# A GpSimd multiplication in the weight load and a two-part moving operand in the expert stage of a decoder layer

## The chip, the core and the metric

The kernel runs on one core of a Trainium2 chip. The time is device microseconds from the first to the last instruction of one execution as the runtime counts them, the median of three runs: 4055.59 us (4050.54 to 4057.15). The engines that matter are TensorE (PE in the profile, its weight loads PEld), VectorE (DVE), ScalarE (ACT), GpSimd (POOL) and the queue of SyncE (SP), which issues most of the loads. ACT and DVE can read the matmul accumulator (PSUM) and SBUF; POOL works here on SBUF alone, and it issues the indirect gathers and scatters of rows.

## What is computed

One decoder layer over 4096 tokens of width 1024. The change lies wholly in its last part, a mixture of 32 experts in which each token goes to two of them:

```
gate  = p_group * p_exp / sum(p_exp)                       # two experts per token
hid   = silu(ragged_dot(xs, w1)) * ragged_dot(xs, w3)      # 1024 -> 512, per expert
ys    = ragged_dot(hid, w2) * gate                         # 512 -> 1024
ffn   = segment_sum(ys, tok)
x     = x + gate2[:, None, :] * ffn                        # gate2 scales the 1024 columns
return rmsnorm(x, final_norm_w)
```

## The kernel before

Four phases run one after the other; only the last, `phase_d` (from about 2600 us on), is touched. Every float32 operand is split into a high part of reduced precision and a remainder (`split`: ACT copies the high part, L71; DVE subtracts, L72), and a product of two operands is three matmuls: high by high, high by low, low by high.

The experts are sorted by token count. Rank r of that order is given a fixed number of rows `CAPS[r]` at build time; what an expert has beyond it is done by a loop at the end whose trip count is found at run time. The order of work alternates ranks from both ends of the list: 0, 31, 1, 30, 2, 29 and so on, ending in the middle. An expert of more than 384 rows is done in chunks of two tiles of 128 rows; all others are one chunk. For the inputs used, ranks 14 to 24 have 235, 203, 200, 200, 186, 172, 171, 168, 151, 136 and 129 tokens (counted from the reference), and before the change each of these eleven had 240 rows.

For each chunk:

- `d_gather` (L1397, POOL) gathers the rows of the next chunk into one of three x buffers; `d_turn` transposes them on PE (L1413) and splits them into `xh` and `xl`.
- `load_expert` brings the weights in twelve blocks of 128x1024: eight of w1 and w3, four of w2. Each is loaded by SP into a raw buffer (L1333; five of these exist), split by ACT into `whD` (L71) and by DVE into `wlD` (L72). The split buffers are a ring of 27 for whatever is in use, and an expert needs 24, so a block can be split only when PE has used up one of the expert before. The four w2 blocks are issued by `load(r, 12)` at the head of the expert's first chunk.
- `d_hidden`: for caps over 128 the weights stand in PE and x moves (L1442 to L1444): four column blocks j, two weights, eight slices k of 128, three products each, 192 in all. Three PSUM buffers take these groups of 24. ACT applies silu to the w1 group (L1447), DVE multiplies by the w3 group (L1448) and the result is split into `hh` and `hl`.
- `d_acc`, `d_to` (POOL): gather of the accumulated rows `ag` from DRAM (L1490) and three small operations for the scatter's row numbers (L1503 to L1505).
- `d_rows`: per 128 rows and half of the 1024 columns twelve matmuls with w2 (L1535 to L1537), then two DVE instructions, `yg = py * gate * g2` (L1542) and `ag = ag + yg` (L1543), then a scatter of `ag` (`keep`, L1570, POOL).
- `d_norm`, `d_root`, `d_out`: one chunk later the finished rows are normalised (DVE L1380) and scattered to the output (L1381, POOL).

A scheduler that runs when the kernel is built sets the order of each engine's queue from its own estimate of times; `self.pin` asks it to keep an instruction in the written order; the rows of the queues below show what came of that. Each engine then works through its queue strictly in order, so an instruction that waits holds back all behind it.

Of the kernel before, what the change touches and what calls it, by code (L numbers as in the profile page):

```python
# [53 lines left out]
class Kern:  # L54
# [1091 lines left out]

    CAPS = [832, 512, 512, 480, 480, 448, 384, 352, 320, 320, 320, 288, 288, 288] + [240] * 11 + [P] * 7
    NC = 384  # L1150

    def phase_d(self):
        tc, nc, T = self.tc, self.nc, self.T
        caps = [min(c, T) for c in self.CAPS]
        with tc.tile_pool(name="D", bufs=2) as p:
# [65 lines left out]
            for i, s in enumerate(st):  # L1221
                nx = st[i + 1] if i + 1 < len(st) else None
                r = s["r"]
                if s["first"]:
                    k = order.index(r)
                    if k + 2 < len(order):
                        load_slots(k + 2)
                    load(r, 12)
                if i == 2:
                    li, limb, col = self.overflow(p, caps)  # L1230
                if nx:
                    self.d_gather(p, nx, ids)

                jobs = []
                if s["last"] and nx:
                    jobs += [lambda: load(nx["r"], 2)] * 4

                pv = st[i - 1] if i else None
                acc = [lambda t=t, m=m: self.d_acc(p, s, t, m, ids) for t, m in s["tiles"]]
                free = self.AGS - (len(pv["tiles"]) if pv else 0)  # L1240
                ends = [acc[:free], acc[free:] + [lambda: self.d_to(p, s, slots)]]
                if pv:
                    ends[0].insert(0, lambda: self.d_norm(p, pv))
                    ends[1].insert(0, lambda: self.d_root(p, pv))
                    ends[1][1:1] = [lambda q=q: self.d_out(p, pv, q) for q in range(len(pv["tiles"]))]
                self.d_hidden(p, s, ex[r], jobs[:2], ends)
                turn = self.d_turn(p, nx) if nx else []
                self.d_rows(p, s, ex[r], slots, turn, jobs[2:], nx is None)
# [78 lines left out]
    def load_expert(self, p, e, w):  # L1327


        nc = self.nc  # L1330

        def block(raw, src, dst, key, n):
            nc.sync.dma_start(raw.rearrange("p (k n) -> p k n", n=n), src)  # L1333
            hi, lo = self.wtile("whD"), self.wtile("wlD")
            self.split(hi[:, 0:1024], lo[:, 0:1024], raw)
            dst[key] = [t[:, 0:1024].rearrange("p (k n) -> p k n", n=n) for t in (hi, lo)]

        for a in range(2):
            for nm, src in (("w1", self.w1), ("w3", self.w3)):
                s = src[0, bass.ds(e, 1)].rearrange("o (k p) n -> p (o k) n", p=P)  # L1340
                for q in range(2):
                    raw = p.tile([P, 1024], F32, name="rawD", bufs=self.RAWS)
                    block(raw, s[:, 4 * q:4 * q + 4, 256 * a:256 * a + 256], w[nm], (a, q), 256)
                    yield
        s = self.w2[0, bass.ds(e, 1)].rearrange("o (k p) n -> p (o k) n", p=P)
        for k in range(4):
# [55 lines left out]
    def d_turn(self, p, s):  # L1402

        nc = self.nc
        s["xh"], s["xl"] = (p.tile([P, KD, self.NC], F32R, name=nm, bufs=1) for nm in ("xh", "xl"))
        steps = []
        o = 0
        for (t, m), x in zip(s["tiles"], s["x"]):
# [12 lines left out]
    def d_hidden(self, p, s, w, jobs, ends):  # L1421
# [11 lines left out]
                    f()  # L1433

        if s["rows"]:
            for j in range(4):
                ph = {}
                for nm in ("w1", "w3"):
                    ph[nm] = self.psum([P, 512], "ph", "pj")[:, 0:n]
                    for k in range(KD):  # L1440
                        hi, lo = (b[:, k % 4, 128 * (j % 2):128 * (j % 2) + 128] for b in w[nm][j // 2, k // 4])
                        nc.tensor.matmul(ph[nm], hi, xh[:, k, 0:n], start=(k == 0), stop=False)  # L1442
                        nc.tensor.matmul(ph[nm], hi, xl[:, k, 0:n], start=False, stop=False)  # L1443
                        nc.tensor.matmul(ph[nm], lo, xh[:, k, 0:n], start=False, stop=(k == KD - 1))  # L1444
                    if nm == "w1":
                        hs = p.tile([P, 512], F32, name="hs", bufs=2)[:, 0:n]
                        nc.scalar.activation(hs, ph[nm], AF.Silu)  # L1447
                nc.vector.tensor_tensor(hs, ph["w3"], hs, op=ALU.mult)  # L1448
                self.split(s["hh"][j][:, 0:n], s["hl"][j][:, 0:n], hs, nc.vector if j == 3 else None)
                if j % 2:  # L1450
                    job()
# [56 lines left out]
    def d_rows(self, p, s, w, slots, turn, jobs, last):  # L1508
# [14 lines left out]
        for q, (t, m) in enumerate(s["tiles"]):  # L1523
# [14 lines left out]

            def add(i):
                cs = slice(512 * i, 512 * i + 512)  # L1540
                yg = p.tile([P, 512], F32, name="yg", bufs=3)[0:m]
                nc.vector.scalar_tensor_tensor(yg, py[i], gate, self.g2[0:m, cs], op0=ALU.mult, op1=ALU.mult)  # L1542
                nc.vector.tensor_tensor(ag[0:m, cs], ag[0:m, cs], yg, op=ALU.add)  # L1543

            if q == 0:

# [73 lines left out]
```

## Time and profile before

| | |
|---|---|
| median of three runs | 4055.59 us |
| the profiled execution, its own time | 4068.07 us |
| its span, first to last instruction | 4066.3 us |
| mean granted TensorE clock | 0.979 |
| busy PE / PEld / DVE / ACT / POOL over the span | 95% / 86% / 63% / 39% / 38% |
| expert stage, 2640 to 4046 us: busy PE / DVE / ACT / POOL | 1364 / 1014 / 626 / 565 us of 1406 |

The profiled execution took 12.5 us more than the median, so differences worked out on it are carried over to the median. The busy shares are averages over stages; in the expert stage PE is busy almost throughout, and DVE is the next.

### The profile page before, as it was taken

Reading aid. Unit: us, or ns where it says so; the run is one execution under the profiler, and the core shown is the slowest. Engines: PE = TensorE matmul, PEld = TensorE weight load, DVE = VectorE, ACT = ScalarE, POOL = GpSimd, SP = SyncE. Lnnn points to the kernel's source line nnn. Section 1 sums busy time; section 2 is a strip of 40 time slices with the busy share of each in tenths; the row PEclk is TensorE's granted clock in tenths of the full one; section 3 lists DMA queues with packets and bytes.
Section 4 is the critical chain, followed back from the end, with each engine's and each line's share of the span. In section 5 each row is a group of like instructions: output and inputs, shape, how many; then the busy total and the mean of one; then the engine's idle time right before and its main releaser. Section 6 shows DMA issues by size and latency. Waiting matters only on the chain.

```text
span 4066.3 us, 72672 instructions
## 1 busy us (share of the span) xinstructions
PE 3853.1 (95%) x26602; PEld 3477.2 (86%) x26602; DVE 2550.0 (63%) x6629; ACT 1602.7 (39%) x3309; POOL 1565.0 (38%) x2195
## 2 busy tenths in 40 slices
PE   5999999999999999979999999599999999999997
PEld 4888888899999999967888888498888889888887
DVE  6655544477777777753444444657777777767786
ACT  3433343444544444432222222224444444444453
POOL 2333333234433443413444444423333443444443
PEclk9999999999999999989999999799999999999999
DMA  6444323422122122356555554446666676666673
GB/s 197 133 135 123 101 76 107 117 60 74 45 68 74 49 67 72 95 160 197 166 169 178 180 170 142 157 134 213 220 215 215 217 238 197 228 202 212 227 241 131
DMA packets 483393, 609.99 MB, mean 150 GB/s; under 512 B 101088, under 2 KB 381384, under 8 KB 483032
## 3 DMA queue, kind: packets, MB, share of 16 engines
q1 hardware_dynamic: 429400, 480.98, 38.4%
q0 software_dynamic: 50592, 118.90, 8.6%
q10 hardware_dynamic: 3040, 5.43, 0.5%
q8 instruction: 211, 3.46, 0.3%
q14 instruction: 150, 1.23, 0.1%
HBM read 475.20 MB, written 183.03 MB: 162 GB/s over the span
## 4 chain that ended last, share of the span: by engine, by line
PE 75%; DMA 9%; DVE 8%; issue 3%; ACT 3%; POOL 1%; SPq 1%; POOLq 0%; DVEq 0%; ACTq 0%
PE ph L1443 5%; PE ph L1444 5%; PE ph L1442 5%; PE pjB L533 4%; PE pjB L534 4%; PE pjB L535 4%; PE py L1535 3%; PE py L1536 3%; PE py L1537 3%; PE poC L298 3%; PE poC L299 3%; PE poC L297 3%; PE pgz L297 3%; PE pgz L299 3%; PE pgz L298 3%
## 5 line engine op out<-in xcount | busy, mean ns | idle before, releaser
L1442 PE MATMUL ph<-xh,whD 128*128 128x240 f32 (+7 forms) x2048 | 580.6, 289 | 14.5 <-DVE ssD L1363 6.5
L1443 PE MATMUL ph<-xl,whD 128*128 128x240 f32 (+7 forms) x2048 | 588.4, 288 | 1.3 <-DVE xl L72 0.8
L1444 PE MATMUL ph<-xh,wlD 128*128 128x240 f32 (+7 forms) x2048 | 586.6, 288 | 0.0
L71 ACT ACTIVATE whD<-rawD 128x1024 fp32r<-128x1024 f32 x384 | 401.3, 1056 | 309.9 <-PE py L1536 127.0
L72 DVE TENSOR_TENSOR wlD<-rawD,whD 128x1024 fp32r<-128x1024 f32 x384 | 460.8, 1218 | 31.2 <-ACT whD L71 30.0
L533 PE MATMUL pjB<-hhB,whi 128*128 128x260 f32 x1536 | 446.2, 293 | 9.9 <-DVE cv L541 5.1
L534 PE MATMUL pjB<-hlB,whi 128*128 128x260 f32 x1536 | 442.8, 289 | 2.6 <-DMA hlB<-hl_d 2.5
L535 PE MATMUL pjB<-hhB,wlo 128*128 128x260 f32 x1536 | 443.5, 289 | 0.0
L1442 PEld LDWEIGHTS ph<-xh,whD 128*128 128x128 f32 x2048 | 388.5, 191 | 20.3 <-ACT xh L71 8.4
L1443 PEld LDWEIGHTS ph<-xl,whD 128*128 128x128 f32 x2048 | 391.1, 191 | 5.9 <-DVE xl L72 3.6
L1444 PEld LDWEIGHTS ph<-xh,wlD 128*128 128x128 f32 x2048 | 391.0, 191 | 1.9
L533 PEld LDWEIGHTS pjB<-hhB,whi 128*128 128x128 f32 x1536 | 292.0, 191 | 14.1 <-ACT beta L410 5.3
L534 PEld LDWEIGHTS pjB<-hlB,whi 128*128 128x128 f32 x1536 | 292.8, 191 | 6.4 <-DMA hlB<-hl_d 3.9
L543 POOL TENSOR_TENSOR cv<-cv,cv 128x256 f32<-128x256 f32 x192 | 141.9, 740 | 405.5 <-DVE Xd L613 142.1
L535 PEld LDWEIGHTS pjB<-hhB,wlo 128*128 128x128 f32 x1536 | 292.8, 191 | 1.6
L1535 PE MATMUL py<-whD,hh 128*128 128x512 f32 (+4 forms) x640 | 258.6, 404 | 12.3 <-ACT hh L71 6.5
L1536 PE MATMUL py<-wlD,hh 128*128 128x512 f32 (+4 forms) x640 | 251.9, 394 | 0.0
L1537 PE MATMUL py<-whD,hl 128*128 128x512 f32 (+4 forms) x640 | 246.0, 400 | 2.9 <-DVE hl L72 2.6
L1570 POOL DMA_INDIRECT acc_d<-ag,to x80 | 111.9, 1399 | 343.1 <-DVE ag L1543 245.7
L541 DVE SCALAR_TENSOR_TENSOR cv<-pjB,cw,cv 128x256 f32<-128x256 f32 x384 | 183.1, 479 | 85.6 <-ACT cv L539 78.5
L299 PE MATMUL pgz<-whi,hlC 128*128 128x512 f32 x512 | 203.8, 398 | 9.7 <-DMA hlC<-hl_d 9.7
L297 PE MATMUL pj<-whi,hh 128*128 128x512 f32 x512 | 205.5, 401 | 6.3 <-ACT whi L71 6.3
(459 smaller groups left out, 10125.9 us busy)
## 6 DMA issues: line engine op xcount, KB each, us to landing
rawD<-in_w_dram SPq DMA_DIRECT2D x384, 512.0 KB, 5.5
wa<-in_w_ada_dram SPq DMA_DIRECT2D x48, 512.0 KB, 4.8
hhB<-hh_d SPq DMA_DIRECT2D x64, 260.0 KB, 4.0
hlB<-hl_d SPq DMA_DIRECT2D x64, 260.0 KB, 4.6
acc_d<-xC SPq DMA_DIRECT2D x32, 520.0 KB, 2.6
wraw<-in_w_in_dram SPq DMA_DIRECT2D x32, 512.0 KB, 6.5
hh_d<-hh SPq DMA_DIRECT2D x16, 1024.0 KB, 7.5
hl_d<-hl SPq DMA_DIRECT2D x16, 1024.0 KB, 10.1
```

The costliest lines, as they stand in the source:

```text
L71: nc.scalar.activation(hi, src, AF.Copy)
L72: (e_lo or nc.vector).tensor_tensor(lo, src, hi.bitcast(F32) if hasattr(hi, "bitcast") else hi, op=ALU.subtract)
L297: nc.tensor.matmul(out, a, hi, start=(k == 0), stop=False)
L299: nc.tensor.matmul(out, b, hi, start=False, stop=(k == KD - 1))
L533: nc.tensor.matmul(pj, wh, hh[k], start=(k == 0), stop=False)
L534: nc.tensor.matmul(pj, wh, hl[k], start=False, stop=False)
L535: nc.tensor.matmul(pj, wl, hh[k], start=False, stop=(k == KD - 1))
L1442: nc.tensor.matmul(ph[nm], hi, xh[:, k, 0:n], start=(k == 0), stop=False)
L1443: nc.tensor.matmul(ph[nm], hi, xl[:, k, 0:n], start=False, stop=False)
L1444: nc.tensor.matmul(ph[nm], lo, xh[:, k, 0:n], start=False, stop=(k == KD - 1))
L1535: nc.tensor.matmul(py[i], a, hi, start=(k == 0), stop=False)
L1536: nc.tensor.matmul(py[i], a, lo, start=False, stop=False)
```

## The change

- The caps of ranks 14 to 24 follow the token counts: one stays at 240, the ten others get 208 to 144.
- Where a chunk with rows on the moving side has at most 208 of them, `xh` and `xl`, now the two halves of one tile `xx`, pass behind the standing high part of the weight in one matmul of 2n columns; the product with the low part keeps n columns. So there are two products per slice instead of three. PSUM then holds two sums side by side; ACT copies the second to SBUF, DVE adds the first to it, and silu and the product read SBUF.
- POOL multiplies each raw w2 block by `g2` before it is split; for that, `d_rows` adds `py * gate` to `ag` in one DVE instruction, and the tile `yg` is gone.
- `load(r, 12)` is written behind the gather of the next chunk.

```
@@ -1146,7 +1146,7 @@
-    CAPS = [832, 512, 512, 480, 480, 448, 384, 352, 320, 320, 320, 288, 288, 288] + [240] * 11 + [P] * 7
+    CAPS = [832, 512, 512, 480, 480, 448, 384, 352, 320, 320, 320, 288, 288, 288] + [240, 208, 208, 208, 192, 176, 176, 176, 160, 144, 144] + [P] * 7
     NC = 384
     def phase_d(self):
@@ -1225,11 +1225,12 @@
                     k = order.index(r)
                     if k + 2 < len(order):
                         load_slots(k + 2)
-                    load(r, 12)
                 if i == 2:
                     li, limb, col = self.overflow(p, caps)
                 if nx:
                     self.d_gather(p, nx, ids)
+                if s["first"]:
+                    load(r, 12)
                 jobs = []
                 if s["last"] and nx:
@@ -1331,6 +1332,9 @@
         def block(raw, src, dst, key, n):
             nc.sync.dma_start(raw.rearrange("p (k n) -> p k n", n=n), src)
+            if n == D:
+                self.pin(nc.gpsimd.tensor_tensor(raw, raw, self.g2, op=ALU.mult))
             hi, lo = self.wtile("whD"), self.wtile("wlD")
             self.split(hi[:, 0:1024], lo[:, 0:1024], raw)
             dst[key] = [t[:, 0:1024].rearrange("p (k n) -> p k n", n=n) for t in (hi, lo)]
@@ -1402,7 +1406,8 @@
     def d_turn(self, p, s):
         nc = self.nc
-        s["xh"], s["xl"] = (p.tile([P, KD, self.NC], F32R, name=nm, bufs=1) for nm in ("xh", "xl"))
+        s["xx"] = p.tile([P, KD, 2, self.NC], F32R, name="xx", bufs=1)
+        s["xh"], s["xl"] = s["xx"][:, :, 0], s["xx"][:, :, 1]
         steps = []
         o = 0
         for (t, m), x in zip(s["tiles"], s["x"]):
@@ -1433,17 +1438,32 @@
                     f()
         if s["rows"]:
+            pair = n <= 208
             for j in range(4):
                 ph = {}
                 for nm in ("w1", "w3"):
-                    ph[nm] = self.psum([P, 512], "ph", "pj")[:, 0:n]
+                    ph[nm] = self.psum([P, 512], "ph", "pj")
+                    two = ph[nm][:, 0:2 * n].rearrange("p (a n) -> p a n", a=2) if pair else None
+                    ph[nm] = ph[nm][:, 0:n]
                     for k in range(KD):
                         hi, lo = (b[:, k % 4, 128 * (j % 2):128 * (j % 2) + 128] for b in w[nm][j // 2, k // 4])
-                        nc.tensor.matmul(ph[nm], hi, xh[:, k, 0:n], start=(k == 0), stop=False)
-                        nc.tensor.matmul(ph[nm], hi, xl[:, k, 0:n], start=False, stop=False)
+                        if pair:
+                            nc.tensor.matmul(two, hi, s["xx"][:, k, :, 0:n], start=(k == 0), stop=False)
+                        else:
+                            nc.tensor.matmul(ph[nm], hi, xh[:, k, 0:n], start=(k == 0), stop=False)
+                            nc.tensor.matmul(ph[nm], hi, xl[:, k, 0:n], start=False, stop=False)
                         nc.tensor.matmul(ph[nm], lo, xh[:, k, 0:n], start=False, stop=(k == KD - 1))
+                    hb = (p.tile([P, 512], F32, name="hs", bufs=2) if nm == "w1" else p.tile([P, 208], F32, name="hb", bufs=1) if pair
+                          else None)
+                    if hb is not None:
+                        hb = hb[:, 0:n]
+                    if pair:
+                        nc.scalar.activation(hb, two[:, 1], AF.Copy)
+                        nc.vector.tensor_tensor(hb, ph[nm], hb, op=ALU.add)
+                        ph[nm] = hb
                     if nm == "w1":
-                        hs = p.tile([P, 512], F32, name="hs", bufs=2)[:, 0:n]
+                        hs = hb
                         nc.scalar.activation(hs, ph[nm], AF.Silu)
                 nc.vector.tensor_tensor(hs, ph["w3"], hs, op=ALU.mult)
                 self.split(s["hh"][j][:, 0:n], s["hl"][j][:, 0:n], hs, nc.vector if j == 3 else None)
@@ -1538,9 +1558,7 @@
             def add(i):
                 cs = slice(512 * i, 512 * i + 512)
-                yg = p.tile([P, 512], F32, name="yg", bufs=3)[0:m]
-                nc.vector.scalar_tensor_tensor(yg, py[i], gate, self.g2[0:m, cs], op0=ALU.mult, op1=ALU.mult)
-                nc.vector.tensor_tensor(ag[0:m, cs], ag[0:m, cs], yg, op=ALU.add)
+                nc.vector.scalar_tensor_tensor(ag[0:m, cs], py[i], gate, ag[0:m, cs], op0=ALU.mult, op1=ALU.add)
             if q == 0:
```

Line numbers move: gather of x L1397 becomes L1401, gather of `ag` L1490 becomes L1510, its scatter L1570 becomes L1588, the output's L1381 becomes L1385, the low product L1444 becomes L1456, w2's products L1535 to L1537 become L1555 to L1557. The multiplication is L1337, the two-part product L1452, the new add L1463.

The first place is POOL's queue around the start of rank 20 (cap 240 before, 176 now), which follows rank 11 (288 rows, three tiles) and comes before rank 12. `acc_d<-ag` is the scatter of a finished tile, `ag<-acc_d` the gather of a new one, `out_dram` the output, `xg` a gather of x. Before:

```order
L1397 DMA xg<-h_d,ids 32x1024
L1570 DMA acc_d<-ag,to 4096x1040 x3
L1490 DMA ag<-acc_d,ids 128x1040
...
L1503 TENSOR_SCALAR to<-ag,slots 112x1
L1397 DMA xg<-h_d,ids 112x1024
...
L1570 DMA acc_d<-ag,to 4096x1040 x2
```

Now:

```order
L1401 DMA xg<-h_d,ids 32x1024
L1337 TENSOR_TENSOR rawD<-rawD,g_28189 128x1024 x4
L1588 DMA acc_d<-ag,to 4096x1040 x3
L1510 DMA ag<-acc_d,ids 128x1040
...
L1401 DMA xg<-h_d,ids 48x1024
L1337 TENSOR_TENSOR rawD<-rawD,g_28189 128x1024 x2
L1525 TENSOR_SCALAR to<-ag,slots 128x1
L1337 TENSOR_TENSOR rawD<-rawD,g_28189 128x1024 x2
...
L1523 TENSOR_SCALAR to<-ag,slots 48x1
L1588 DMA acc_d<-ag,to 4096x1040
```

The four multiplications for rank 20's w2 stand ahead of the three scatters of rank 11, and the four for rank 12's w2 stand ahead of the first scatter of rank 20, among its small operations.

The second place is PE's queue at the end of rank 20's hidden stage, where the last products of `ph` meet the transposes (`ptx`) and the first products with w2 (`py`; `hh` with the lowest number is j = 0). Before:

```order
L1442 MATMUL ph<-xh,whD 128x240
L1443 MATMUL ph<-xl,whD 128x240
L1444 MATMUL ph<-xh,wlD 128x240
L1413 MATMUL ptx<-K,xg 128x128 x8
L1535 MATMUL py<-whD,hh_41049 128x512
L1536 MATMUL py<-wlD,hh_41049 128x512
L1537 MATMUL py<-whD,hl_41053 128x512
L1535 MATMUL py<-whD,hh_41050 128x512
L1536 MATMUL py<-wlD,hh_41050 128x512
```

Now:

```order
L1452 MATMUL ph<-xx,whD 128x352
L1456 MATMUL ph<-xx,wlD 128x176
L1555 MATMUL py<-whD,hh_41600 128x512
L1556 MATMUL py<-wlD,hh_41600 128x512
L1555 MATMUL py<-whD,hh_41600 128x512
L1556 MATMUL py<-wlD,hh_41600 128x512
L1557 MATMUL py<-whD,hl_41604 128x512 x2
L1452 MATMUL ph<-xx,whD 128x352
```

The first products with w2 now stand among the hidden products, with two more column groups of 16 still behind them; before, they stood behind the last hidden product.

## Rows read from the trace of the kernel before

**Rows 1.** Windows: length, busy PE, PEld, DVE, ACT, POOL, clock, DMA share, GB/s

```profile
2640.00:4046.00 1406.00, 1364.38 (x9296) 1242.65 (x9294) 1013.76 (x1817) 625.63 (x936) 564.68 (x622) 0.99 0.64 209
3690.00:3708.00 18.00, 17.94 (x104) 14.27 (x103) 9.10 (x16) 1.35 (x3) 7.54 (x17) 1.00 0.37 124
3708.00:3741.00 33.00, 31.95 (x229) 27.84 (x228) 30.23 (x54) 20.09 (x31) 14.29 (x12) 1.00 0.79 260
```

**Rows 2.** PE's waits, 2640 to 4066: us in total, times, longest

```profile
PE ptx L1413 <- DVE xl L72: 10.3, 12, 1.5
...
PE plst L1320 <- DVE xl L72: 0.3, 1, 0.3
```

**Rows 3.** Timeline of PE, four widths: start and duration in us

```profile
3365.27 0.27 PE L1443 MATMUL ph<-xl,whD 128*128 128x240 f32 x1
...
3367.40 0.27 PE L1444 MATMUL ph<-xh,wlD 128*128 128x240 f32 x1
...
3183.14 0.27 PE L1444 MATMUL ph<-xh,wlD 128*128 128x192 f32 x1
...
3184.81 0.28 PE L1444 MATMUL ph<-xh,wlD 128*128 128x192 f32 x1
...
3830.71 0.29 PE L1444 MATMUL ph<-xh,wlD 128*128 128x288 f32 x1
...
3833.75 0.29 PE L1444 MATMUL ph<-xh,wlD 128*128 128x288 f32 x1
...
3245.30 0.34 PE L1444 MATMUL ph<-xh,wlD 128*128 128x384 f32 x1
...
3248.28 0.34 PE L1444 MATMUL ph<-xh,wlD 128*128 128x384 f32 x1
```

**Rows 4.** Groups of instructions: count, busy us, mean ns, idle before

```profile
L72 DVE TENSOR_TENSOR wlD<-rawD,whD 128x1024 fp32r<-128x1024 f32 x384 | 460.8, 1218 | 31.2 <-ACT whD L71 30.0
...
L1542 DVE SCALAR_TENSOR_TENSOR yg<-py,slots,g 128x512 f32<-128x512 f32 (+4 forms) x160 | 116.4, 747 | 133.6 <-PE py L1537 133.1
...
L1543 DVE TENSOR_TENSOR ag<-ag,yg 128x512 f32<-128x512 f32 (+4 forms) x160 | 107.6, 686 | 7.5 <-DMA ag<-acc_d,ids 3.8
...
L994 POOL TENSOR_TENSOR h2C<-h2C,B 128x1024 f32<-128x1024 f32 x31 | 74.2, 2395 | 39.6 <-DVE h2C L993 21.2 <-PE poC L299 8.8 <-DVE ohg L1026 3.9
```

**Rows 5.** Groups by shape: the steps behind a hidden group

```profile
L1448 DVE TENSOR_TENSOR hs<-ph,hs 128x224 f32<-128x224 f32 x8 | 3.1, 387 | 4.8 <-PE ph L1444 4.8
...
L1447 ACT ACTIVATE hs<-ph 128x192 f32<-128x192 f32 x4 | 1.3, 322 | 0.4 <-PE ph L1444 0.4
```

**Rows 6.** Timeline of the phase before, POOL and DVE

```profile
1976.37 2.40 POOL L994 TENSOR_TENSOR h2C<-h2C,B 128x1024 f32<-128x1024 f32 x1 [1.47 <-PE poC L299]
...
1976.82 3.10 DVE L72 TENSOR_TENSOR ml<-tr,mh 128x512 fp32r<-128x512 f32 x2 [0.60 <-ACT mh L71]
...
2002.18 1.28 DVE L72 TENSOR_TENSOR ml<-tr,mh 128x512 fp32r<-128x512 f32 x2
...
2178.02 1.29 POOL L947 TENSOR_TENSOR mix<-mix,sg 128x512 f32<-128x512 f32 x1 [3.87 <-ACT sg L940]
...
2178.76 1.29 DVE L979 TENSOR_TENSOR xC<-poC,xC 128x512 f32<-128x512 f32 x2 [0.45 <-DMA xC<-in_x_dram]
```

**Rows 7.** Timeline: a held POOL, a late scatter, a gap on PE

```profile
3658.70 4.58 POOL L1505 TENSOR_SCALAR to<-ag,slots 112x1 int32<-112x1 f32 x1
...
3671.12 1.28 DVE L1380 SCALAR_TENSOR_TENSOR ag<-ag,ssD,fw 128x1024 f32<-128x1024 f32 x1 [3.85 <-DMA acc_d<-ag,to]
...
3678.82 0.55 PE L1442 MATMUL ph<-xh,whD 128*128 128x288 f32 x1 [3.65 <-DVE ssD L1363]
```

**Rows 8.** Timeline of SP and ACT around w2, and loads to landing

```profile
3686.27 4.15 SPq L1333 DMA_DIRECT2D rawD<-in_w_dram  x4
...
3708.24 2.01 ACT L71 ACTIVATE whD<-rawD 128x1024 fp32r<-128x1024 f32 x2 [3.45 <-PE py L1536]
...
rawD<-in_w_dram SPq DMA_DIRECT2D x384, 512.0 KB, 5.5
```

More of the change, by code (lines that the diff above doesn't have):

```diff
@@ L1145, in sort @@
         v.tensor_scalar(eid, eid, -1.0, float(NE - 1), op0=ALU.mult, op1=ALU.add)
-    CAPS = [832, 512, 512, 480, 480, 448, 384, 352, 320, 320, 320, 288, 288, 288] + [240] * 11 + [P] * 7
+    CAPS = [832, 512, 512, 480, 480, 448, 384, 352, 320, 320, 320, 288, 288, 288] + [240, 208, 208, 208, 192, 176, 176, 176, 160, 144, 144] + [P] * 7
     NC = 384
@@ L1227, in phase_d @@
                         load_slots(k + 2)
-                    load(r, 12)
                 if i == 2:
@@ L1232, in phase_d @@
                     self.d_gather(p, nx, ids)
+                if s["first"]:
+                    load(r, 12)
                 jobs = []
@@ L1333, in block @@
             nc.sync.dma_start(raw.rearrange("p (k n) -> p k n", n=n), src)
+            if n == D:
+                self.pin(nc.gpsimd.tensor_tensor(raw, raw, self.g2, op=ALU.mult))
             hi, lo = self.wtile("whD"), self.wtile("wlD")
@@ L1404, in d_turn @@
         nc = self.nc
-        s["xh"], s["xl"] = (p.tile([P, KD, self.NC], F32R, name=nm, bufs=1) for nm in ("xh", "xl"))
+        s["xx"] = p.tile([P, KD, 2, self.NC], F32R, name="xx", bufs=1)
+        s["xh"], s["xl"] = s["xx"][:, :, 0], s["xx"][:, :, 1]
         steps = []
@@ L1435, in d_hidden @@
         if s["rows"]:
+            pair = n <= 208
             for j in range(4):
@@ L1438, in d_hidden @@
                 for nm in ("w1", "w3"):
-                    ph[nm] = self.psum([P, 512], "ph", "pj")[:, 0:n]
+                    ph[nm] = self.psum([P, 512], "ph", "pj")
+                    two = ph[nm][:, 0:2 * n].rearrange("p (a n) -> p a n", a=2) if pair else None
+                    ph[nm] = ph[nm][:, 0:n]
                     for k in range(KD):
                         hi, lo = (b[:, k % 4, 128 * (j % 2):128 * (j % 2) + 128] for b in w[nm][j // 2, k // 4])
-                        nc.tensor.matmul(ph[nm], hi, xh[:, k, 0:n], start=(k == 0), stop=False)
-                        nc.tensor.matmul(ph[nm], hi, xl[:, k, 0:n], start=False, stop=False)
-                        nc.tensor.matmul(ph[nm], lo, xh[:, k, 0:n], start=False, stop=(k == KD - 1))
+                        if pair:
+                            nc.tensor.matmul(two, hi, s["xx"][:, k, :, 0:n], start=(k == 0), stop=False)
+                        else:
+                            nc.tensor.matmul(ph[nm], hi, xh[:, k, 0:n], start=(k == 0), stop=False)
+                            nc.tensor.matmul(ph[nm], hi, xl[:, k, 0:n], start=False, stop=False)
+                        nc.tensor.matmul(ph[nm], lo, xh[:, k, 0:n], start=False, stop=(k == KD - 1))
+                    hb = (p.tile([P, 512], F32, name="hs", bufs=2) if nm == "w1" else p.tile([P, 208], F32, name="hb", bufs=1) if pair
+                          else None)
+                    if hb is not None:
+                        hb = hb[:, 0:n]
+                    if pair:
+                        nc.scalar.activation(hb, two[:, 1], AF.Copy)
+                        nc.vector.tensor_tensor(hb, ph[nm], hb, op=ALU.add)
+                        ph[nm] = hb
                     if nm == "w1":
-                        hs = p.tile([P, 512], F32, name="hs", bufs=2)[:, 0:n]
+                        hs = hb
                         nc.scalar.activation(hs, ph[nm], AF.Silu)
@@ L1540, in add @@
                 cs = slice(512 * i, 512 * i + 512)
-                yg = p.tile([P, 512], F32, name="yg", bufs=3)[0:m]
-                nc.vector.scalar_tensor_tensor(yg, py[i], gate, self.g2[0:m, cs], op0=ALU.mult, op1=ALU.mult)
-                nc.vector.tensor_tensor(ag[0:m, cs], ag[0:m, cs], yg, op=ALU.add)
+                nc.vector.scalar_tensor_tensor(ag[0:m, cs], py[i], gate, ag[0:m, cs], op0=ALU.mult, op1=ALU.add)
             if q == 0:
```

## The prediction

> **What bounds the kernel now.** I read the windows of the expert stage first, then PE's waits, then PE's timeline for the price of one product, then DVE's and POOL's groups, and last the timelines of single places. In the windows PE is busy 1364 of the stage's 1406 us at a granted clock of 0.99, DVE 1014, ACT 626, POOL 565 [rows 1]. PE's waits list ten kinds; from 10.3 us for the transposes behind DVE down to 0.3 they sum to 40 us [rows 2]. So the stage goes at PE's pace, and PE's pace is the number of its products. The timeline prices them by the distance of starts: at 240 columns 20 starts span 2.13 us (19 steps, 112.1 ns each), at 192 columns 15 steps take 1.67 us (111.3 ns). Twenty per cent fewer columns change nothing: there is a floor. At 288 columns 23 steps take 3.04 us (132.2 ns), at 384 17 steps take 2.98 us (175.3 ns): above the floor a column costs 0.449 ns [rows 3].
>
> **The two-part product.** Per slice k an expert of cap 240 pays three products at the floor, 3 x 112.1 = 336 ns. The new one pays one product of 2n columns and one of n at the floor, 111.3 ns. From the two wide rows: 2n = 288 costs 132.2 ns, 320 146.6, 352 160.9, 384 175.3, and 416, just past them, 189.7 [rows 3]. The difference per slice is 225.0 ns less that: 92.8, 78.4, 64.1, 49.7 and 35.3 ns. An expert has 4 x 2 x 8 = 64 slices, so it saves 5.9, 5.0, 4.1, 3.2 and 2.3 us; there are 2, 1, 3, 1 and 3 experts of these caps: 11.9 + 5.0 + 12.3 + 3.2 + 6.8 = **39 us** of PE, all on the path. No row shows a moving operand in two pieces; one-piece rows are the nearest, and the other end is no gain at all (a rival below). Narrower caps alone would give PE nothing, by the floor.
>
> The Trainium skill, "TensorE: Matmul & The Clock Gate", section "Back-to-back issue gap", gives the distance of isolated products as N/2.4 + 2.5 ns. By it 192 columns would cost 82.5 ns, three apart and two joined would differ by one 2.5 ns only, and the whole gain would be 640 x 2.5 ns = 1.6 us. The 111.3 ns at 192 columns and 112.1 at 240 disagree [rows 3]; the same page's section "LDWEIGHTS" has 128/1.2 = 107 ns for the weights of one product, which is near the floor.
>
> **The price of the two sums.** For ten experts and eight groups each, 80 groups, ACT gains a copy (0.322 us at 192 columns) and DVE an add (0.387 at 224) [rows 5]: 26 us of ACT, 31 of DVE. PSUM of a group is released after both, about 0.7 us, instead of after one. Three buffers let PE run two groups ahead, each 8 x (0.16 + 0.11) = 2.2 us, so mostly it is covered; if the cover were gone it would be 80 x 0.7 = 56 us. In the second place of the queues PE also gets the first w2 products to run while the last groups are turned. I take +4 us; the bounds are 0 and 56.
>
> **One DVE instruction instead of two.** L1543 goes, 160 x 0.686 = 107.6 us of DVE; the remaining one has the form of L1542 and I leave its 0.747 us [rows 4]. With the adds DVE loses about 77 us net. On the path this can return only what PE waits for, at most the 40 us of [rows 2]. DVE's crowd is local: in the 33 us in which rank 20 runs it is busy 30.2, in the 18 before it 9.1 [rows 1]. I take -6, bounds -40 and 0.
>
> **POOL's multiplication.** The nearest row has its very shape: 128x1024 times a row tile, 2.395 us [rows 4]; 4 x 32 = 128 of them are 307 us, for an engine that has 1406 - 565 = 841 idle. Time on POOL is not the price; two other things are. The first is that POOL and DVE hold each other up. A DVE pair with both inputs in SBUF that starts 0.45 us into a 2.40 us multiplication takes 3.10 us instead of 1.28: it stands until POOL ends, 1.82 us more. A DVE pair with an input in PSUM, in the same position, takes 1.29 as alone [rows 6]. So the new single add and the xl splits go through, while `wlD`, `hl` and the small steps of the norm are held. With 128 multiplications this is 0 to 128 x 1.82 = 233 us of DVE. Where do they fall? Rank 20's last w2 blocks are loaded from 3686.3 on, land 5.5 us later and wait until 3708.2 for buffers that PE still reads [rows 8]; their multiplications stand ahead of rank 11's scatters in the queue, so they fall into the half-idle 18 us [rows 1]. The other four, for the next large expert, fall into or behind the crowded 33 us, mostly where DVE reads PSUM. I charge a fifth of the remaining 64 x 1.82 = 116 us, rounded down: 20 us, less some slack of PSUM: +12. Bounds 0 and 116.
>
> The second thing is the queue. Behind each group of four stand scatters, then gathers of `ag` that wait for them. Rank 20's first scatter now waits for rank 12's w2 to land and for up to 9.6 us of multiplications. Who waits for it is seen in the profile: POOL held 4.58 us in a tiny step, the scatter late, DVE's L1380 waiting 3.85 us for the scatter to land, and PE standing 3.65 us because DVE, stuck there, does not empty PSUM [rows 7]. In the new DVE order that output step stands one column group later, which gives about 6 us back (48 products of 132 ns, [rows 3]). So I charge nothing here and keep it as the slower rival. The moved `load(r, 12)` issues four loads on SP and four splits per expert later in the text, but SP's queue waits on free raw buffers anyway; the first tiles of the next x stay ahead of the multiplications in POOL's queue.
>
> **Caps.** All eleven counts lie below their caps, so the run-time loop still has no trip; its trip count is the check that the change does what it says. Fewer rows in gathers and splits are worth some tenths of a microsecond on engines that wait; nothing.
>
> **Sum.** -39 + 4 - 6 + 12 = -29. On the profiled execution, 4068.1 (span 4066.3 and 1.8 around it), that is 4039; it lies 12.5 above the median, so against 4055.6 I predict **4027**.
>
> **Rivals.**
> - *The waits go too.* The DVE time saved empties the crowd and POOL's holds fall in gaps: -39 and half of the 40 us, 4055.6 - 39 - 20 = 3997. For it: the crowded windows are short. Against: those windows hold most two-SBUF steps.
> - *Half is lost again.* DVE is held in the crowd for 30 us or more, or PSUM comes late in the paired groups: 4055.6 - 39 + 35 = 4052. For it: 30.2 of 33 us; against: PE's two groups of slack.
> - *The late scatter, slower.* Multiplications ahead of a scatter repeat the 3.65 us gap in each of the 17 turns of a large expert after a small one: 62 us, so 4055.6 - 39 + 4 - 6 + 62 = 4077. It decides once the scatter of the smaller expert lands after PE has used its three PSUM buffers, about 19 us into the next hidden stage (144 products of 132 ns). For it: the gap is there already; against: the later place of L1380's step.
> - *Two pieces cost what two products cost.* Then -39 is gone and the rest stays: 4055.6 + 4 - 6 + 12 = 4066. For it: no row; against: PSUM and x are read in plain strides.
>
> **How the numbers follow.** Forecast (4010 to 4045) 0.56; waits go too 0.12; half lost 0.16; late scatter 0.11; two pieces 0.05. A measurement of this kernel tells about 0.2%, 8 us, from no change: faster is below 4047.5, slower above 4063.7. Faster takes the first two and half of the third: 0.76. The same takes the rest of the third and a little of the two last: 0.11. Slower 0.13. The range runs from 4000 to 4061: it cuts the lowest end of the second case and most of the last two, some 0.2.
>
> **What would show it.** PE starts 161 ns apart behind a 352-column product and 111 ns behind a 176-column one, and the hidden stage of a 176 expert at about 17.4 us instead of 21.5 where nothing interrupts it. L1337 at 2.4 us x128, in gaps of DVE for the small experts' half. `wlD` above 1.218 us on average, up to 1.8. PE's waits at 40 us give or take 20. The prediction is wrong if 352 columns start 224 ns apart, if PE's waits pass 80 us with the scatter or `ag` at their root, or if `wlD`'s mean passes 2 us.

## The result, and the profile after

The changed kernel took **4192.91 us** (median of 4 runs, 4189.21 to 4199.11) against 4056.37 us (4 runs, 4050.54 to 4062.18): ratio 1.0335, 95% interval 1.0317 to 1.0352. It is slower by some 136 us, where 4027 us, about 29 us faster, was forecast.

The profiled execution has a span of 4197.0 us, 130.7 more than before. The windows of the changed kernel, with the columns of [rows 1]; the first is the stage of before cut at the same times, the second the whole stage as it is now:

```profile
2640.00:4046.00 1406.00, 1255.45 (x7827) 1116.09 (x7826) 985.34 (x1573) 578.64 (x913) 783.25 (x676) 0.94 0.58 191
2639.00:4179.00 1540.00, 1375.05 (x8494) 1219.90 (x8492) 1088.00 (x1741) 638.13 (x1019) 859.98 (x746) 0.94 0.58 189
```

In [rows 1] PE was busy 97% of the stage at a clock of 0.99. Now it is busy 89% of it at 0.94, and with 802 fewer rows of products than before (704 fewer in the program) it is busy 11 us longer. POOL is busy 295 us more, the multiplications.

PE's waits in the changed kernel, 2639 to 4179 us (in total, times, longest), the largest of the list that answers to [rows 2]:

```profile
PE ptx L1418 <- DVE xx L72: 39.2, 19, 7.4
PE py L1555 <- DVE hh L69: 37.8, 16, 7.3
PE py L1557 <- DVE hl L72: 21.1, 10, 4.0
PE ph L1455 <- DVE xx L72: 13.6, 4, 4.7
PE ph L1454 <- DVE hs L1468: 11.8, 6, 4.9
PE py L1555 <- ACT hh L71: 11.0, 11, 2.2
```

Nearly all of them end with DVE. From the first product with w2 to the last they sum to 163 us, against 40.5 before. Neither the scatter nor the gather of `ag` is named among them; that says only what came last, and the second timeline below has a scatter in the chain behind one of them. Why DVE is late is seen at one place, in the timeline of the changed kernel around 3143 us (start and duration in us, PE, DVE and POOL):

```profile
3140.13 0.39 PE L1557 MATMUL py<-whD,hl 128*128 128x512 f32 x1
3140.36 0.39 PE L1555 MATMUL py<-whD,hh 128*128 128x512 f32 x1
...
3142.23 8.81 DVE L72 TENSOR_TENSOR wlD<-rawD,whD 128x1024 fp32r<-128x1024 f32 x1
...
3143.00 6.95 POOL L1337 TENSOR_TENSOR rawD<-rawD,g 128x1024 f32<-128x1024 f32 x3
...
3150.96 0.26 DVE L69 CAST hh<-hs 128x224 fp32r<-128x224 f32 x1
...
3151.28 0.79 PE L1555 MATMUL py<-whD,hh 128*128 128x512 f32 x1 [7.29 <-DVE hh L69]
...
3151.87 0.63 PE L1556 MATMUL py<-wlD,hh 128*128 128x512 f32 x1
...
3152.30 0.63 PE L1555 MATMUL py<-whD,hh 128*128 128x512 f32 x1
...
4148.66 9.75 DVE L1376 TENSOR_SCALAR ssD<-ssD 128x2 f32<-128x2 f32 x1 [0.17 <-ACT jkD L1370]
...
4149.00 9.37 POOL L1337 TENSOR_TENSOR rawD<-rawD,g 128x1024 f32<-128x1024 f32 x4
```

Read it from the middle. A split that takes 1.22 us by itself stands on DVE for 8.81 us, until three multiplications on POOL, one behind the other, are over. The cast of `hh` waits behind it in DVE's queue, PE waits 7.29 us for the cast, and then goes on with starts 0.43 us apart in place of 0.23. The granted clock was 1.00 from 3140 to 3143 us and is 0.50 from 3151 to 3155: of its two levels, 1.2 and 2.4 GHz, the lower one. The last two rows show the same with the smallest of operations, two columns, held for 9.75 us by four multiplications.

Here and below "held" is the sum, over DVE's instructions from POOL's first multiplication to the last product with w2, of what each takes beyond the quick ones (shortest fifth) of its operation and shape, from 0.3 us up. It is 0.3 us before (from the first product with w2) and **179 us in 62 instructions** now, the longest 9.6; each of the 62 lies beside a multiplication. (The expectations below have 187 us: that counts two casts, 8 us, which stand ahead of the first multiplication and are as slow in the kernel before. The 139 us that they have for e12 are 134 by this count.) "Slow starts" sums, roughly, what PE's products start later than their usual distance where PE waited for nothing: 12.7 us before, 57.2 now. From the first product with w2 to the last the stage takes 1394.7 us before and 1538.4 now. Of these 143.7 us, 123 are waits and 45 slow starts, and the two-part product gives 42 back by the distances of its starts; some 18 are not assigned. The stage starts 11.5 us earlier than before and what follows it takes 1.5 us less, which leaves the 130.7.

Not every wait of PE goes back to a held DVE. The changed kernel around 3800 us, where no step of DVE is held while PE waits or in the 15 us before:

```profile
3779.80 0.74 DVE L1561 SCALAR_TENSOR_TENSOR ag<-py,slots,ag 128x512 f32<-128x512 f32 x1
...
3788.25 9.55 POOL L1337 TENSOR_TENSOR rawD<-rawD,g 128x1024 f32<-128x1024 f32 x4
...
3797.97 1.84 POOL L1588 DMA_INDIRECT acc_d<-ag,to  x1 [0.17 <-issue]
...
3814.57 1.62 POOL L1588 DMA_INDIRECT acc_d<-ag,to  x1 [7.28 <-DVE wlD L72]
...
3819.30 1.27 DVE L1384 SCALAR_TENSOR_TENSOR ag<-ag,ssD,fw 32x1024 f32<-32x1024 f32 x1 [2.69 <-DMA acc_d<-ag,to]
...
3822.68 1.97 PE L1418 MATMUL ptx<-K,xg 128*128 128x128 f32 x8 [7.37 <-DVE xx L72]
```

The first tile of `ag` is done at 3780.5. Its scatter starts behind four multiplications, at 3798, and the last of the three scatters follows at 3814.6. DVE's output step waits 2.69 us for a scatter to land, and behind it stands the x split for which PE waits 7.37 us. Five waits of PE, 28.8 us together, have DVE waiting for a scatter inside them, for 10 us in all; in the kernel before none has.

The product itself came out as forecast. PE's timeline of the changed kernel, places for 176 tokens:

```profile
3700.40 0.35 PE L1452 MATMUL ph<-xx,whD 128*128 128x352 f32 x1
3700.59 0.24 PE L1456 MATMUL ph<-xx,wlD 128*128 128x176 f32 x1
3700.67 0.35 PE L1452 MATMUL ph<-xx,whD 128*128 128x352 f32 x1
```

0.19 and 0.08 us between starts, 0.27 together, where 160.9 + 111.3 = 272 ns were worked out from [rows 3]. The groups that answer to [rows 4] (count, busy us, mean ns, idle before):

```profile
L1337 POOL TENSOR_TENSOR rawD<-rawD,g 128x1024 f32<-128x1024 f32 x128 | 313.6, 2471 | 36.3 <-DMA rawD<-in_w_dram 9.4 <-DVE hl L72 8.2 <-DVE hs L1468 7.8
...
L72 DVE TENSOR_TENSOR wlD<-rawD,whD 128x1024 fp32r<-128x1024 f32 x384 | 535.9, 1406 | 68.4 <-ACT whD L71 65.4 <-PE ph L1492 0.8 <-PE py L1556 0.2
...
L1561 DVE SCALAR_TENSOR_TENSOR ag<-py,slots,ag 128x512 f32<-128x512 f32 (+7 forms) x160 | 116.3, 745 | 198.5 <-PE py L1557 182.4 <-DMA ag<-acc_d,ids 13.0 <-issue 3.0
```

POOL's time and the single addition (745 ns against 747) are as forecast too. The mean of `wlD` rose only from 1218 to 1406 ns: a mean over 384 hides 23 that took two to nine microseconds.

### The profile page after: what moved, and what is told of

It is laid out like the page before. It is cut to its first block, busy times and chain, and to the rows that moved or that the text cites. A ratio compares the mean times of both kernels' runs of the same rounds, so it can differ in the third digit from the quotient of the medians.

```text
span 4197.0 us, 71480 instructions
## 1 busy us (share of the span) xinstructions
PE 3871.1 (92%) x25898; PEld 3463.4 (83%) x25898; DVE 2633.3 (63%) x6562; ACT 1617.3 (39%) x3397; POOL 1867.8 (45%) x2323
## 5 line engine op out<-in xcount | busy, mean ns | idle before, releaser
L72 DVE TENSOR_TENSOR wlD<-rawD,whD 128x1024 fp32r<-128x1024 f32 x384 | 535.9, 1406 | 68.4 <-ACT whD L71 65.4
L1456 PE MATMUL ph<-xx,wlD 128*128 128x256 f32 (+11 forms) x2048 | 572.0, 281 | 0.0
L1455 PE MATMUL ph<-xx,whD 128*128 128x256 f32 (+6 forms) x1344 | 398.3, 297 | 13.6 <-DVE xx L72 13.6
L1454 PE MATMUL ph<-xx,whD 128*128 128x256 f32 (+6 forms) x1344 | 396.1, 300 | 13.3 <-DVE hs L1468 11.8
L1456 PEld LDWEIGHTS ph<-xx,wlD 128*128 128x128 f32 x2048 | 399.5, 195 | 3.8
L1337 POOL TENSOR_TENSOR rawD<-rawD,g 128x1024 f32<-128x1024 f32 x128 | 313.6, 2471 | 36.3 <-DMA rawD<-in_w_dram 9.4
L1555 PE MATMUL py<-whD,hh 128*128 128x512 f32 (+6 forms) x640 | 268.6, 420 | 54.6 <-DVE hh L69 37.8
L1454 PEld LDWEIGHTS ph<-xx,whD 128*128 128x128 f32 x1344 | 260.8, 196 | 18.5 <-DVE hs L1468 13.3
L1455 PEld LDWEIGHTS ph<-xx,whD 128*128 128x128 f32 x1344 | 260.5, 194 | 17.2 <-DVE xx L72 15.5
L1557 PE MATMUL py<-whD,hl 128*128 128x512 f32 (+6 forms) x640 | 254.2, 416 | 21.5 <-DVE hl L72 21.1
L1556 PE MATMUL py<-wlD,hh 128*128 128x512 f32 (+6 forms) x640 | 260.9, 408 | 0.0
L1588 POOL DMA_INDIRECT acc_d<-ag,to x80 | 127.5, 1593 | 256.7 <-DVE ag L1561 119.3
L1561 DVE SCALAR_TENSOR_TENSOR ag<-py,slots,ag 128x512 f32<-128x512 f32 (+7 forms) x160 | 116.3, 745 | 198.5 <-PE py L1557 182.4
```

The lines of the kernel that those rows point to most:

```text
L72: (e_lo or nc.vector).tensor_tensor(lo, src, hi.bitcast(F32) if hasattr(hi, "bitcast") else hi, op=ALU.subtract)
L1337: self.pin(nc.gpsimd.tensor_tensor(raw, raw, self.g2, op=ALU.mult))
L1555: nc.tensor.matmul(py[i], a, hi, start=(k == 0), stop=False)
L1556: nc.tensor.matmul(py[i], a, lo, start=False, stop=False)
L1557: nc.tensor.matmul(py[i], b, hi, start=False, stop=(k == 3))
```

## The experiments

The theories. **H**: POOL's multiplication holds DVE, and PE waits for DVE. **Q**: what waits for the multiplications or stands behind them in a queue is late (w2's splits on ACT, POOL's gathers and scatters). **P**: the sums that the two-part product needs cost it its gain. An expectation that uses another letter says what it stands for. All runs at a glance (us; PE's waits, slow starts and held as above):

| run | time | against before, 95% | waits | slow starts | held |
|---|---|---|---|---|---|
| before | 4056 to 4061 | 1 | 41 | 13 | 0 |
| changed | 4193 | 1.0317 to 1.0352 | 163 | 57 | 179 |
| e1_pair_only | 4059 | 0.9988 to 1.0010 | 63 | 31 | 0 |
| e2_g2_only | 4149 | 1.0196 to 1.0241 | 101 | 37 | 165 |
| e3_no_mult | 4038 | 0.9933 to 0.9969 | 50 | 18 | 0 |
| e4_one_input | 4076 | 1.0023 to 1.0068 | 75 | 27 | 64 |
| e5_aside | 4168 | 1.0247 to 1.0315 | 134 | 44 | 149 |
| e6_pieces | 4188 | 1.0289 to 1.0334 | 157 | 53 | 113 |
| e7_pair_no_sum | 4026 | 0.9897 to 0.9946 | 45 | 17 | 0 |
| e8_caps_only | 4051 | 0.9965 to 0.9993 | 40 | 12 | 0 |
| e9_dve_mult | 4117 | 1.0129 to 1.0160 | 102 | 40 | 0 |
| e10_pair_reduce | 4041 | 0.9944 to 0.9973 | 51 | 21 | 0 |
| e11_reduce_176 | 4050 | 0.9969 to 0.9995 | 55 | 20 | 0 |
| e12_aside_own_tile | 4123 | 1.0125 to 1.0186 | 107 | 38 | 134 |
| e13_one_by_one | 4152 | 1.0201 to 1.0251 | 110 | 57 | 156 |
| e14_four_raw | 4141 | 1.0179 to 1.0240 | 128 | 37 | 158 |
| e15_no_mult_four_raw | 4058.5 | 0.9982 to 1.0006 | 65 | 19 | 0 |
| e16_reduce_four_raw | 4046 | 0.9957 to 0.9980 | 60 | 24 | 0 |

**The change in its two halves.** e1 is the changed kernel with gate2 as before; e2 is the kernel before with the lines of gate2, without the two-part product and its places.

```
e1  - self.pin(nc.gpsimd.tensor_tensor(raw, raw, self.g2, op=ALU.mult))   (L1542, L1543 and load(r, 12) as before)
e2  + self.pin(nc.gpsimd.tensor_tensor(raw, raw, self.g2, op=ALU.mult))   (with the single addition, load(r, 12) later)
```

> Only the two-part product and its smaller places for 129 to 208 tokens; gate2 stays on DVE behind w2 and w2's last four blocks are loaded where they were before. Theory H (DVE's operations are held while POOL multiplies; 186 us of DVE time by the trace of the changed kernel): nothing is held, so the forecast's own terms hold, 4056 - 39 + 4 = 4021 us (4000 to 4045). Theory Q (what stands behind the multiplications, ACT's splits of w2 and POOL's gathers and scatters, comes late): the same 4021. Theory P (the two-part product's extra sum and later release of PSUM cost the 136 us): 4100 or more.

> Only gate2 into w2's columns by POOL, the single addition behind w2, and the later place of the load of w2; products and places as in the kernel before. H and Q: all of the loss and none of the 35 us that the product saves, 4193 + 35 = 4228 us (4190 to 4260). P: below 4080.

Gate2 alone costs 90 us (net of the addition that is gone from DVE), the product alone gives nothing, together they cost 136. That a PE with shorter products has less behind which a late DVE can hide would fit this; no run shows it. The size expected for e2 (4228) is missed by 80 us; H, Q and P all had part of it wrong, since none had the two halves add to more than their sum.

**The multiplication taken out, or made one of a single input.**

```
e3  - self.pin(nc.gpsimd.tensor_tensor(raw, raw, self.g2, op=ALU.mult))
e4  + self.pin(nc.gpsimd.tensor_scalar(raw, raw, 1.0, None, op0=ALU.mult))   (in its place)
```

> The changed kernel without POOL's multiplication, so gate2 is left out of the experts' rows; the rest as it is. H and Q: 4021 less the second operation that is gone from DVE behind w2 (6 us as forecast), about 4015 us (3985 to 4045). P: 4100 or more.

> The changed kernel with POOL's operation on each w2 block made one of a single tensor input (the block times the constant 1.0, so gate2 is left out), at the same place in POOL's queue and with w2's splits waiting for it as before. H: an operation of one tensor input doesn't hold DVE, so within 40 us of the run without the multiplication, 4015 to 4055 us, and DVE held under 20 us in all. Q: the queue and the waits are the same, so 4150 to 4195 us if the operation is about as long as the multiplication.

Without it the kernel is 155 us quicker than with it. e4 has the same queue and the same waits, and an operation on POOL that is even longer, 2.86 us on average against 2.47. It costs 38 us, not 155. So Q, as the main cause, is out. H's time was missed by 21 us (4076, where 4015 to 4055 was expected), and its reason was wrong: the operation of one input holds DVE too, 64 us in 67 instructions, none by more than 1.7. The timeline of e4:

```profile
3039.64 2.31 DVE L72 TENSOR_TENSOR wlD<-rawD,whD 128x1024 fp32r<-128x1024 f32 x1 [1.87 <-ACT whD L71]
...
3039.80 8.28 POOL L1337 TENSOR_SCALAR rawD<-rawD 128x1024 f32<-128x1024 f32 x3
...
3041.87 1.76 DVE L445 SCALAR_TENSOR_TENSOR ssD<-rb_t,rb_y 128x2 f32<-128x2 f32 x1
```

A split of 1.22 us takes 2.31 and a two-column step 1.76, but DVE gets its turn while POOL's three go on.

**The multiplication beside the path.** Its product goes to a spare tile, so that nothing waits for it; in e12 that tile is its own.

```
e5   junk = p.tile([P, 1024], BF, name="junk", tag="yg", bufs=3); ...tensor_tensor(junk, raw, self.g2, op=ALU.mult)
e12  junk = p.tile([P, 1024], BF, name="junk", bufs=1)   (jkD then has two buffers of its own)
```

> The changed kernel with POOL's product of w2 block and gate2 written to a spare tile that nobody reads (bf16), so that w2's splits take the block as it landed and don't wait for POOL; gate2 is left out of the rows. POOL is as busy as before. H (DVE held): nearly all of the loss stays, DVE held 120 us or more, 4130 to 4195 us. Q (w2's splits wait for POOL and ACT's queue with them): what is left over the run without the multiplication (4038 us) is small, 4040 to 4080 us.

> As the run with the product written aside (4168 us), but the spare tile is its own: there it shared buffers with the scratch of ACT's squares for the norm, which waited 65 us for POOL in 12 places. Here neither w2's splits nor that step of ACT wait for POOL; POOL is as busy, gate2 is left out. H (DVE held): DVE held 130 us or more and 4110 to 4170 us, over half of the 155 us that lie between the run without the multiplication (4038) and the changed kernel (4193). Q (ACT's steps waiting for POOL): 4040 to 4080 us.

e5 stays at 4168, but in it ACT's squares for the norm waited 65 us for POOL, which speaks neither for nor against. In e12 none of ACT's waits in the stage names POOL, and 84 of the 155 us are still there, with 134 us held. POOL's queue is as full as before, and a raw buffer still comes free only when POOL has read it; but e4 has both and costs 38 us. So over half of the loss stays with the hold as its main source left: H is shown for that part. In e12's timeline two multiplications, the second of which waits for the first to be done, take 5.87 us, and DVE gets a turn between them:

```profile
3446.75 5.87 POOL L1338 TENSOR_TENSOR junk<-rawD,g 128x1024 bf16<-128x1024 f32 x2
...
3447.71 6.00 DVE L72 TENSOR_TENSOR wlD<-rawD,whD 128x1024 fp32r<-128x1024 f32 x2
```

No single operation is held for more than 3 us here, against 9.6 in the changed kernel, whose multiplications run in rows of up to four.

**Shorter pieces, one at a time, fewer raw buffers.** Is it then the length of the holds?

```
e6   for c in range(0, 1024, 256): ...tensor_tensor(raw[:, c:c + 256], raw[:, c:c + 256], self.g2[:, c:c + 256], op=ALU.mult)
e13  RAWS = 4; w2g = p.tile([P, 1024], F32, name="w2g", bufs=1); ...tensor_tensor(w2g, raw, self.g2, op=ALU.mult); raw = w2g
e14  RAWS = 4
```

> The changed kernel, each multiplication in four pieces of 256 columns, one behind the other. H1: a held DVE operation gets its turn between two of POOL's operations; each hold is then at most about 0.6 us, DVE held 187 / 4 = 47 us in all, and the time 4038 + 47 = 4085 us (4060 to 4110). H2: the hold lasts as long as POOL has two-input operations one behind the other; DVE held as before (150 to 200 us), 4170 to 4220 us. Q: the same as the changed kernel or longer, 4190 to 4230 us.

> The changed kernel, POOL's multiplication written to one tile of its own (four raw buffers in place of five, for its room), so that each multiplication waits until DVE has split the block before: w2's splits wait for POOL as in the changed kernel, but no two multiplications run without a pause. B (the length of the holds: DVE is not let in between two multiplications that are both ready): no hold over 2.6 us, DVE held about as in the run with the tile of its own aside (139 us), 4120 to 4150 us. Q (the 70 us between that run, 4123, and the changed kernel come from the splits that wait for POOL): 4190 us or more, since they now wait longer.

> The changed kernel with four raw buffers in place of five, the control of the run in which each multiplication waits for the one before. B and Q: the price of the buffer alone, 0 to 30 us over the changed kernel, 4193 to 4223 us.

In e6 most holds (88 of 102) are under 1 us, yet seven exceed 5 us, and POOL takes 904 ns for a quarter, 446 us in all against 314; the time is that of the changed kernel, with a third less held. H2 had that time, but with 150 to 200 us held; no theory had both. In e13 every multiplication stands alone and no hold passes 3.1 us, but 156 us are held in all and it is no quicker than its control e14. So B falls: rows of multiplications are not what the rest of the loss hangs on. And the control went the other way than both theories had it, 52 us quicker than the changed kernel.

**Four raw buffers without the multiplication.** The same edit, `RAWS = 4`, in e3 and in e10 (below).

> The run without the multiplication (4038 us; gate2 left out), with four raw buffers in place of five. F (four buffers are quicker by themselves, whatever POOL does, since w2's loads of the next turn start later): 3985 to 4010 us, the same 52 us as in the changed kernel. T (four buffers only move where the multiplications fall on DVE): 4030 to 4060 us, no gain.

> The two-part product alone with the DVE reduction (4041 us), with four raw buffers. F: 3990 to 4015 us. T: 4035 to 4060 us.

T: four buffers are not quicker by themselves (20 and 5 us slower). Against e15 the multiplication costs 4141 - 4058.5 = 83 us in e14 and 93 in e13. Put beside what was held, the price of a held microsecond is 38/64 = 0.59 in e4, 84/134 = 0.63 in e12, 83/158 = 0.53 in e14 and 93/156 = 0.60 in e13, but 155/179 = 0.86 in the changed kernel, 130/149 = 0.87 in e5 and 149/113 = 1.32 in e6. So held time does not account for all of the loss. At 0.5 to 0.6, near what added work on DVE itself costs (e9, below), the 179 us of the changed kernel make 90 to 107 of its 155.

Of the other 48 to 65 us the scatters are one part: DVE's wait for them takes 10 us of PE's waits in the changed kernel, and at most 3 in any other run with POOL's operation. The splits that wait for POOL are hardly the rest: ACT waits 122 us for them in the changed kernel, but also 112 in e4, 134 in e14 and 225 in e13. What remains (where the holds fall, which five buffers and four place differently, would be one guess) is **left open**.

**The same work on DVE.**

```
e9  nc.vector.tensor_tensor(raw, raw, self.g2, op=ALU.mult)   (in place of nc.gpsimd)
```

> The changed kernel with the multiplication of w2's blocks by gate2 on DVE, whose splits of a block of this size take 1.22 us: 128 x 1.22 = 156 us of DVE time, less than the 187 us for which DVE was held by POOL. H: the loss follows the DVE time that is taken away, 0.83 us per us as in the changed kernel, and no operation is longer than its own work: 4038 + 0.83 x 156 = 4168 us as the upper end, 4100 as the lower, since these 1.22 us come one by one and not in holds of up to 9.6 us; in any case below the changed kernel's 4193. Q (queue behind the multiplications): the splits of w2 wait for the same product in DVE's queue, so no better than 4190.

DVE does 155.1 us more work (128 of 1217 ns), nothing is held, and the kernel is at 4117, within H's 4100 to 4168: 79 us over e3, 0.51 per us, and 76 us quicker than with the work on POOL.

**The sums.** e7 leaves the sums out; e8 has the places alone; e10 makes the sum in one DVE operation, for e11 only up to 176 places.

```
e7   - nc.scalar.activation(hb, two[:, 1], AF.Copy)
     - nc.vector.tensor_tensor(hb, ph[nm], hb, op=ALU.add)
e8   + CAPS = [..., 240, 208, 208, 208, 192, 176, 176, 176, 160, 144, 144] + [P] * 7   (kernel before)
e10  + nc.vector.tensor_reduce(hb, two.rearrange("p a n -> p n a"), axis=AX.X, op=ALU.add)   (for the two lines of e7)
e11  + pair = n <= 176   (e10, else)
```

> The two-part product alone (as in the first of these runs, 4059 us), without the ACT copy and DVE addition that put its two halves together: the low part of x is left out of the hidden rows, each half's product still runs. P (the sums and the later release of PSUM eat the 35 us): about 4021 us (4010 to 4035). R (with shorter products the turn runs at the pace of ACT and DVE, whose other work is unchanged): 4045 to 4060 us.

> The kernel before with the smaller places for 129 to 208 tokens and nothing else. Products of 144 to 208 columns start as far apart as those of 240 (111 ns), so P and R both expect no gain on PE: 4050 to 4060 us. S (another order of instructions by the scheduler, or the smaller places, cost time by themselves): 4080 or more.

> The two-part product alone, its two halves put together by one DVE reduction that reads both from PSUM, in place of an ACT copy and a DVE addition: one handover and 88 ACT copies of 0.33 us less. P (the sums' cost is the chain ACT, DVE, ACT and PSUM's release behind it): between the run with the copy and the addition and the one without sums, 4059 to 4026; 4040 us (4030 to 4050). R (any sum costs the same DVE time): 4055 to 4065.

> The run with the DVE reduction (4041 us), but the two-part product only for experts of up to 176 places; those of 192 and 208 keep three products. Per pair of products the distances of the starts are 222 ns less 189.7 (208 places) or 175.3 (192): 64 slices x 32 ns x 3 experts + 64 x 47 x 1 = 9 us of PE time given up, for 32 sums the fewer (4 experts x 8). P (a sum costs 33 us / 88 with copy and addition, about 0.2 us with the reduction): 4041 + 9 - 6 = 4044 us (4036 to 4052). R (where the sums are what holds the turn): below 4036.

P, and the size is the one expected: 4059 - 4026 = **33 us** for 88 sums. What the sum is made of, from the groups of e1 (0.31 and 0.34 us, where [rows 5] gave 0.32 and 0.39) and then of e10:

```profile
L1459 DVE TENSOR_TENSOR hb<-ph,hb 128x176 f32<-128x176 f32 (+4 forms) x44 | 14.8, 336 | 3.9 <-ACT hb L1458 3.7
...
L1458 ACT ACTIVATE hb<-ph 128x176 f32<-128x176 f32 (+4 forms) x44 | 13.6, 310 | 8.3 <-PE ph L1452 7.1 <-DVE hs L1459 0.9
```

```profile
L1458 DVE TENSOR_REDUCE hb<-ph 128x176 f32<-128x352 f32 (+4 forms) x44 | 23.0, 522 | 2.5 <-PE ph L1452 2.5
```

And PE's wait for the PSUM of the transposes to be emptied, its largest in e1, in e1, e7 and e10, 2640 to 4050 us:

```profile
PE ptx L1414 <- DVE xx L72: 26.9, 18, 3.8
```

```profile
PE ptx L1414 <- DVE xx L72: 7.3, 11, 1.7
```

```profile
PE ptx L1414 <- DVE xx L72: 13.8, 12, 2.6
```

One reduction of 0.52 us takes more of DVE than the addition of 0.34, but without the copy on ACT and the handover it gives 18 us back. e10, in which every sum is made, beats both kernels: 0.9958 of the time before. By e11 the product is worth it up to 208 places: giving up 9 us of PE time there cost about 9, and the sums that fell away gave nothing back that shows.

## Why the prediction was wrong

**The step that failed** is POOL's multiplication: "I charge a fifth of the remaining 64 x 1.82 = 116 us, rounded down: 20 us, less some slack of PSUM: +12. Bounds 0 and 116." The multiplication cost 155 us (e3 against the changed kernel), beyond the upper bound, and both factors were too small. *How many steps are held*: the half of the 128 that belongs to the small experts was to fall into half-idle stretches, for nothing, and a fifth of the other 64, some 13, was charged. Held were 29 instructions beside the first half, 80 us, and 33 beside the second, 99 us. *How long*: the 1.82 us of [rows 6], a hold that ends with the one multiplication beside it, was taken for the longest. But a step can stand through a whole row of multiplications, and only 25 of the 128 stand alone: 19 of the 62 holds are over 2.6 us, up to 9.6, and make 102 of the 179 us. The kernel before has such a hold, in rows that the prediction did not read:

```profile
2602.95 4.45 DVE L1298 CAST ef<-sw 128x32 f32<-128x32 int32 x1
...
2603.67 3.69 POOL L1488 MEMSET ag<- 128x1040 f32 x4
```

A cast of the same shape takes 0.18 us 5 us later; this one stands until four operations on POOL are over.

That the small steps of the norm are held was forecast. What stands behind any held step was not priced: all of DVE's queue, with the casts and PSUM releases that PE waits for. And the waits cost PE again in clock, +45 us of slow starts, which no term of the sum had.

The Trainium skill, "SBUF — State Buffer", section "Who interferes with whom", says that a DVE operation with two SBUF inputs contends with a GpSimd operation that reads SBUF, and that whoever issues first keeps the shared ports for its whole instruction. The trace agrees that they contend, for POOL's operation of two inputs (179 us held) and of one (64 us, e4). That a DVE operation may stand through several POOL instructions, 8.81 us for three, is longer than that sentence has it; and that one starts in the trace 0.77 us ahead of POOL's first and is held all the same.

**The other terms.** *The two-part product, -39*: right in its distances; eleven groups of tokens take it, not ten, since the last 192 of the places for 448 tokens do too, which makes 42. Without the sums the kernel with it is 33 us quicker than before (e7), of which the smaller places alone may be 8 (e8), where nothing was forecast for them; so 25 to 33 of the 42 were paid out. *The sums, +4, bounds 0 and 56*: mis-sized; 33 us. The sums stand in the queues of ACT and DVE ahead of the x splits, and these release PE's transposes: that wait is 26.9 us in e1 and 7.3 in e7. *L1543 gone, -6, bounds -40 and 0*: e3 against e1 has -21, with the later load. *The queue behind the multiplications, 0*: too low. No wait of PE is put down to a scatter or to `ag` from DMA directly, but the rival of the late scatter did happen, by the very chain that it names (3788 to 3823 us above): DVE's output steps wait 58.5 us for scatters, 36.0 before, and five waits of PE, 28.8 us, contain such a wait, where the rival had 62. It is the smaller part; e4, with the queue as it was, needs no more than its held time to explain it. "Half is lost again" had the right place, DVE held in the crowd, and put at 35 us what cost 155. The premise that a step of DVE with an input in PSUM goes through was right: none of the 62 held instructions reads PSUM, and the 73 that do and lie beside a multiplication for most of their time took 0.75 us at most.

**The tests that it set.** PE's waits over 80 us came true, with the root named, the scatter, behind five of them alone. `wlD`'s mean under 2 us would have passed the forecast: the mean over all blocks was the wrong test, the longest row the right one.

Split by e3, the 136 us found are -21 (the product, the sums and L1543 together, e3 against before) and +155 (the multiplication). That the two add up is no check; they meet in the same run.

## What to carry to other kernels

Work moved to an idle POOL is not free for a busy DVE: look up how long DVE's operations that read SBUF alone would stand beside it, count rows of POOL operations as one hold, ask what stands behind them in POOL's own queue, and compare with doing the work on DVE itself, which here was 76 us quicker. What a shorter product on PE saves is paid out only if the engines that feed it and empty its PSUM have the time; count each new operation in their queues by what stands behind it. A wait of some microseconds on PE costs more than its length where the clock falls with it.

## What was not expected of the hardware

- POOL's operation of one fp32 input, 128x1024 times a constant, holds DVE as well, 64 us over 128 of them, at most 1.7 us each; on two inputs 179 us, at most 9.6.
- DVE's steps with a single input are held too: the cast `hh` on 128x256 took 2.42 us in place of 0.3 at 2830 us of the changed kernel.
- A DVE operation on 128x2 stood 9.75 us for four multiplications of 9.37 us. Where the second multiplication had to wait for the first to be done, DVE got its turn between them (5.87 us for two).
- After 7.29 us without work PE's products with w2 started 0.43 us apart at a granted clock of 0.50, before it 0.23 at 1.00.
- One raw buffer less moved the changed kernel by 52 us, and the same kernel without the multiplication by 20 the other way.
